# The first four batches spread over all 128 partitions, one batch per step, with their softmax through TensorE

## The chip, the core and the metric

The kernel runs on one core of a Trainium2 chip. The metric is the device time of one execution in microseconds; the time before is the median of three runs. The profile is one further execution, taken by the hardware profiler, with every instruction and every DMA packet recorded.

## What is computed

For each of 8 batches the reference takes two matrices of 4096 rows and 512 columns, both float32, forms the dot product of row i of `x` with row i of `y`, and takes the softmax of these 4096 numbers:

```python
# x, y: (8, 4096, 512) float32
gram = np.matmul(x, y.transpose(0, 2, 1))
diag = np.diagonal(gram, axis1=1, axis2=2)      # only row i with row i is used
diag = diag - diag.max(axis=-1, keepdims=True)
exp = np.exp(diag)
return exp / exp.sum(axis=-1, keepdims=True)    # (8, 4096)
```

So 134.2 MB have to be read (two inputs of 67.1 MB), each number is used once, and 0.13 MB are written.

## The kernel before

**Tiling.** The 8 batches are handled in two halves of four. In each half, partition p belongs to batch p // 32 (a quadrant of 32 partitions for each batch) and holds 128 consecutive rows of it; the starts of two neighbouring partitions lie 128 rows, 256 KB, apart in memory. A step loads 32 of these 128 rows on every partition: 64 KB per partition, 8 MB of `x` and 8 MB of `y`. Four steps make a half; there are S = 8 steps (t = 0 to 7). Column c of the tile `diag[i]` (128 x 128) takes the dot products of half i.

**Buffers.** `x` goes in turn into two tiles `xs0` and `xs1`; `y` has one tile `ys`, and a small tile `side` into which ScalarE copies the last K = 6 rows of `ys` (L123), so that they can be overwritten earlier.

**A step (L118 to L131).** The loads of `x` (L63) and `y` (L66) are issued from the queue of SyncE (SP). VectorE (DVE) multiplies the first 26 rows by `ys` (L70, 128x13312), then the last 6 by `side` (L70, 128x3072), both in place in `xs`. Then VectorE adds up 30 of the 32 products per partition (L73) and ScalarE the other two (L78). In step 0 the `x` load is cut in two: 2 rows per partition first, then 30.

**What sets the order.** The schedule is written by hand: each engine runs its instructions in the order of the source. SP runs the loads in that order too, and a load waits on SP until its buffer is free: the `x` load of step t + 2 until the sums of step t are done, the `y` load of step t + 1 until VectorE's first product of step t and the copy into `side` are done. SP's DMAs use eight completion semaphores in turn, so that a DMA can also wait for the one eight places before it. A DMA is split over 16 DMA engines, 8 partitions each; each engine works through its descriptors in the order of issue. One partition's contiguous run is one packet in the trace.

**Softmax of the first half.** After step 3, `exps` (L99) takes the largest of 128 columns (L97), the largest of each quadrant by a transposing reduction (L91), and lets ScalarE take the exponentials with their sum (L104). In step 4, ahead of its products, `normalize` (L107) adds up over the quadrant (L91), takes the reciprocal (L110) and scales (L111). TensorE has no work at all.

**The end.** Steps 6 and 7 are cut finer: in step 6 `y` comes in two parts of 16 rows, step 7 comes in parts of 16, 8, 4, 2, 1 and 1 rows, with multiply and sum in one VectorE instruction per row (`dots`, L83). Behind the last loads SP issues four DMAs of 16 KB with the result of the first half (L156). Then come the softmax of the second half and its output DMA of 64 KB, on ScalarE's queue (L158).

Of the kernel before, what the change touches and what calls it, by code (L numbers as in the profile page):

```python
# [1 line left out]

# [5 lines left out]


@with_exitstack
def kernel(
    ctx: ExitStack,
    tc: tile.TileContext,
    x: bass.AP,
    y: bass.AP,
    out: bass.AP,
):
    nc = tc.nc
    ctx.enter_context(tc.manual_schedule())  # L20
    f32 = mybir.dt.float32
    Alu = mybir.AluOpType
    Act = mybir.ActivationFunctionType
    X = mybir.AxisListType.X
    B, N, D = x.shape
    P = nc.NUM_PARTITIONS
    G = 32
    Q = P // G
    C = N // G
    R = 32  # L30
    H = R // 2
    K = 6
    W = 2
    S = B // Q * (C // R)


    xv = x.rearrange("(s b) (j c) d -> s (b j) c d", b=Q, j=G)
    yv = y.rearrange("(s b) (j c) d -> s (b j) c d", b=Q, j=G)
    ov = out.rearrange("(s b) (j c) -> s (b j) c", b=Q, j=G)

    big = ctx.enter_context(tc.tile_pool(name="big", bufs=1))
    small = ctx.enter_context(tc.tile_pool(name="small", bufs=1))


    xs = [big.tile([P, R, D], f32, name=f"xs{i}") for i in range(2)]
    ys = big.tile([P, R, D], f32, name="ys")
    side = big.tile([P, K, D], f32, name="side")

    diag = [small.tile([P, C + i], f32, name=f"diag{i}") for i in range(B // Q)]
    res = [small.tile([P, C], f32, name=f"res{i}") for i in range(B // Q)]  # L50

    def columns(t, r0, n):
        c0 = t % (C // R) * R + r0
        return slice(c0, c0 + n)

    def rows(t, r0, n):
        return xs[t % 2][:, r0 : r0 + n, :]

    def dots_of(t, r0, n):
        return diag[t * R // C][:, columns(t, r0, n)]  # L60

    def load_x(t, r0, n):
        nc.sync.dma_start(out=rows(t, r0, n), in_=xv[t * R // C, :, columns(t, r0, n), :])  # L63

    def load_y(t, r0, n):
        nc.sync.dma_start(out=ys[:, r0 : r0 + n, :], in_=yv[t * R // C, :, columns(t, r0, n), :])  # L66

    def products(t, r0, n, yt):
        xt = rows(t, r0, n)
        nc.vector.tensor_tensor(out=xt, in0=xt, in1=yt, op=Alu.mult)  # L70

    def sums(t, r0, n):
        nc.vector.tensor_reduce(out=dots_of(t, r0, n), in_=rows(t, r0, n), axis=X, op=Alu.add)  # L73

    def sums_act(t, r0, n):
        for r in range(r0, r0 + n):
            row = xs[t % 2][:, r, :]
            nc.scalar.activation(out=row, in_=row, func=Act.Copy, accum_out=dots_of(t, r, 1))  # L78

    def dots(t, r0, n):  # L80
        for r in range(r0, r0 + n):
            xt = xs[t % 2][:, r, :]
            nc.vector.scalar_tensor_tensor(  # L83
                out=xt, in0=xt, scalar=1.0, in1=ys[:, r, :], op0=Alu.mult, op1=Alu.mult,
                accum_out=dots_of(t, r, 1),
            )

    def over_quadrant(name, column, op, negate=False):

        got = small.tile([P, 1], f32, name=name)  # L90
        nc.vector.tensor_reduce(  # L91
            out=got, in_=column.to_broadcast([P, G]), axis=X, op=op, negate=negate, apply_transpose=True
        )
        return got

    def largest(out, d):
        nc.vector.tensor_reduce(out=out, in_=d, axis=X, op=Alu.max)  # L97

    def exps(i, d):  # L99
        mxp = small.tile([P, 1], f32, name=f"mxp{i}")  # L100
        largest(mxp, d)
        nmx = over_quadrant(f"nmx{i}", mxp, Alu.max, negate=True)
        sump = small.tile([P, 1], f32, name=f"sump{i}")
        nc.scalar.activation(out=res[i], in_=diag[i][:, :C], func=Act.Exp, bias=nmx, scale=1.0, accum_out=sump)  # L104
        return sump

    def normalize(i, sump):  # L107
        total = over_quadrant(f"sum{i}", sump, Alu.add)
        rc = small.tile([P, 1], f32, name=f"rc{i}")
        nc.vector.reciprocal(out=rc, in_=total)  # L110
        nc.vector.tensor_single_scalar(out=res[i], in_=res[i], scalar=rc, op=Alu.mult)  # L111

    nc.vector.addr_align(128, offset=0, max_nops=0)
    nc.scalar.addr_align(128, offset=0, max_nops=0)

    for t in range(S - 2):  # L118
        if t == 0:
            load_x(t, 0, 2)  # L120
        load_x(t, 2 if t == 0 else 0, R - 2 if t == 0 else R)
        load_y(t, 0, R)
        nc.scalar.activation(out=side, in_=ys[:, R - K :, :], func=Act.Copy)  # L123
        if t == C // R:
            normalize(0, sump)
        products(t, 0, R - K, ys[:, : R - K, :])
        products(t, R - K, K, side)
        sums(t, 0, R - W)
        sums_act(t, R - W, W)
        if t == C // R - 1:  # L130
            sump = exps(0, diag[0])  # L131

    t = S - 2
    load_x(t, 0, R)
    for r0 in (0, H):
        load_y(t, r0, H)
        products(t, r0, H, ys[:, r0 : r0 + H, :])
    sums(t, R - H // 2, H // 2)
    sums_act(t, 0, R - H // 2)

    t += 1
    r0 = 0
    for n in (16, 8, 4, 2, 1, 1):
        if r0 < R - 1:
            load_x(t, r0, max(n, 2))
        load_y(t, r0, n)
        if r0 == R - 2:
            largest(diag[1][:, C:], diag[1][:, : C - 2])
        dots(t, r0, n)
        r0 += n  # L150

    met = small.tile([P, C - R], f32, name="met")
    nc.scalar.activation(out=met, in_=diag[1][:, : C - R], func=Act.Copy)  # L153

    for p, n in ((0, G), (G, G), (2 * G, G), (3 * G, G)):
        nc.sync.dma_start(out=ov[0, p : p + n, :], in_=res[0][p : p + n, :])  # L156
    normalize(1, exps(1, diag[1][:, C - 2 :]))
    nc.scalar.dma_start(out=ov[1], in_=res[1])  # L158


# [1 line left out]
_INS = ['x', 'y']  # L162
_OUTS = [((8, 4096), 'float32')]


# [23 lines left out]
```

## Time and profile before

| | |
|---|---|
| time, median of 3 runs | 320.74 us (320.57 to 320.8) |
| profiled execution: span from the first to the last recorded event | 318.9 us |
| VectorE busy | 244.7 us (77%) |
| ScalarE busy | 42.0 us (13%) |
| TensorE | no instruction of the kernel |
| DMA queue of SP (q1) | 4080 packets, 134.29 MB, 97.8% of 16 engines' span |
| DMA queue of ScalarE (q10) | 144 packets, 0.07 MB, 0.1% |
| HBM read | 134.22 MB, 421 GB/s over the span |

The profiled execution has a span of 318.9 us; the time of a run is measured around it, and its median lies 1.8 us above the span. In the profile's lines, "x8" is a number of instructions, "busy, mean ns" their summed and mean duration, and an arrow "<-" names what ended a wait. "SPq" is SyncE's queue, where DMAs are issued. The "chain that ended last" follows the work back from the last instruction, at each step to what released it.

### The profile page before, as it was taken

To read this page: it belongs to the slowest core of one execution; us is meant where nothing else is said; L and a number is where in the kernel's file an instruction comes from. 1 tells how busy PE (TensorE), PEld (TensorE's weight loads), DVE (VectorE), ACT (ScalarE), POOL (GpSimd) and SP (SyncE) were. 2 spreads that over 40 slices of the span, in tenths; PEclk is the share of its full clock that TensorE was granted. 3 is DMA by queue.
4 is the path that set the end of the run, shared out by engine and by line. 5 is a ranking of instruction groups with operands and counts; after the bars stand their busy time and mean duration, and the time that the engine had idled before them with its cause. 6 is when DMAs were issued, how large, how long until landed. Compare 5 with 4: busy or idle time off the path is not lost.

```text
span 318.9 us, 304 instructions
## 1 busy us (share of the span) xinstructions
DVE 244.7 (77%) x96; ACT 42.0 (13%) x84; POOL 0.2 (0%) x4
## 2 busy tenths in 40 slices
DVE  0000069995899939999399994999949999996995
ACT  1000030100301003010120103000030100197000
POOL 0000000000000000000000000000000000000000
DMA  8989999999999999999999999999999899999993
GB/s 314 493 378 485 436 395 436 485 395 403 510 403 395 477 444 395 427 493 395 403 510 403 395 460 460 395 419 493 403 395 510 358 444 415 444 423 419 421 413 116
DMA packets 4226, 134.37 MB, mean 421 GB/s; under 512 B 512, under 2 KB 768, under 8 KB 1536
## 3 DMA queue, kind: packets, MB, share of 16 engines
q1 hardware_dynamic: 4080, 134.29, 97.8%
q10 hardware_dynamic: 144, 0.07, 0.1%
q14 instruction: 2, 0.02, 0.0%
HBM read 134.22 MB, written 0.13 MB: 421 GB/s over the span
## 4 chain that ended last, share of the span: by engine, by line
DMA 62%; DVE 35%; issue 2%; SPq 0%; ACT 0%; DVEq 0%
DMA ys<-in_y_dram 62%; DVE xs L70 30%; DVE diag L73 4%; DVE xs L83 0%; SPq L63 0%; DVE res L111 0%; DVE nmx L91 0%; DVE sum L91 0%; ACT res L104 0%; DVE rc L110 0%; DVE mxp L97 0%; DVEq L70 0%; SPq L66 0%; DVEq L83 0%
## 5 line engine op out<-in xcount | busy, mean ns | idle before, releaser
L70 DVE TENSOR_TENSOR xs<-xs,ys 128x13312 f32<-128x13312 f32 (+1 forms) x8 | 101.4, 12690 | 66.5 <-DMA ys<-in_y_dram 66.5
L73 DVE TENSOR_REDUCE diag<-xs 128x30 f32<-128x15360 f32 (+1 forms) x7 | 101.3, 14477 | 0.2
L78 ACT ACTIVATE xs<-xs 128x512 f32<-128x512 f32 x36 | 22.2, 616 | 111.0 <-DVE xs L70 111.0
L123 ACT ACTIVATE side<-ys 128x3072 f32<-128x3072 f32 x6 | 16.6, 2764 | 124.0 <-DMA ys<-in_y_dram 124.0
L83 DVE SCALAR_TENSOR_TENSOR xs<-xs,ys 128x512 f32<-128x512 f32 x32 | 19.9, 686 | 3.3 <-DMA ys<-in_y_dram 3.3
L70 DVE TENSOR_TENSOR xs<-xs,side 128x3072 f32<-128x3072 f32 x6 | 20.1, 3351 | 0.0
L78 ACT ACTIVATION_READ_ACCUMULATOR xs<-xs 128x1 f32 x36 | 6.7, 186 | 0.0
L104 ACT ACTIVATE res<-diag,nmx 128x128 f32<-128x128 f32 x2 | 0.8, 402 | 37.6 <-DVE nmx L91 37.6
L83 DVE DVE_READ_ACCUMULATOR xs<-xs,ys 128x1 f32 x32 | 2.6, 81 | 0.0
L123 ACT ACT_TABLE_LOAD x1 | 1.3, 1283 | 1.2 <-PEq L173 1.2
L91 DVE TRANSPOSE_TENSOR_REDUCE sum<-sump 128x1 f32<-128x32 f32 x2 | 0.4, 212 | 1.2 <-ACT res L104 1.2
L111 DVE TENSOR_SCALAR res<-res,rc 128x128 f32<-128x128 f32 x2 | 0.6, 286 | 0.1
L97 DVE TENSOR_REDUCE mxp<-diag 128x1 f32<-128x128 f32 (+1 forms) x2 | 0.4, 220 | 0.1
L91 DVE TRANSPOSE_TENSOR_REDUCE nmx<-mxp 128x1 f32<-128x32 f32 x2 | 0.4, 212 | 0.1
L110 DVE RECIPROCAL rc<-sum 128x1 f32<-128x1 f32 x2 | 0.3, 164 | 0.1
L104 ACT ACTIVATION_READ_ACCUMULATOR res<-diag,nmx 128x1 f32 x2 | 0.4, 186 | 0.0
L97 DVE TENSOR_REDUCE diag<-diag 128x1 f32<-128x126 f32 x1 | 0.3, 284 | 0.1
L153 ACT ACTIVATE met<-diag 128x96 f32<-128x96 f32 x1 | 0.3, 282 | 0.0
L173 POOL MEMSET const-bfloat16-1.0<- 128x1 bf16 x1 | 0.1, 102 | 0.0
L173 POOL MEMSET const-uint8-127<- 128x1 uint8 x1 | 0.1, 102 | 0.0
L173 POOL MEMSET const-float32-0.0<- 128x1 f32 x1 | 0.1, 99 | 0.2 <-issue 0.2
L173 POOL MEMSET const-float32-1.0<- 128x1 f32 x1 | 0.1, 99 | 0.0
## 6 DMA issues: line engine op xcount, KB each, us to landing
ys<-in_y_dram SPq DMA_DIRECT2D x3, 4096.0 KB, 16.0
xs<-in_x_dram SPq DMA_DIRECT2D x1, 7680.0 KB, 21.8
xs<-in_x_dram SPq DMA_DIRECT2D x1, 4096.0 KB, 14.9
xs<-in_x_dram SPq DMA_DIRECT2D x1, 2048.0 KB, 20.5
ys<-in_y_dram SPq DMA_DIRECT2D x1, 2048.0 KB, 17.2
xs<-in_x_dram SPq DMA_DIRECT2D x3, 512.0 KB, 22.1
xs<-in_x_dram SPq DMA_DIRECT2D x1, 1024.0 KB, 19.3
ys<-in_y_dram SPq DMA_DIRECT2D x1, 1024.0 KB, 21.3
```

The costliest lines, as they stand in the source:

```text
L70: nc.vector.tensor_tensor(out=xt, in0=xt, in1=yt, op=Alu.mult)
L73: nc.vector.tensor_reduce(out=dots_of(t, r0, n), in_=rows(t, r0, n), axis=X, op=Alu.add)
L78: nc.scalar.activation(out=row, in_=row, func=Act.Copy, accum_out=dots_of(t, r, 1))
L83: nc.vector.scalar_tensor_tensor(out=xt, in0=xt, scalar=1.0, in1=ys[:, r, :], op0=Alu.mult, op1=Alu.mult, accum_out=dots_of(t, r, 1),)
L91: nc.vector.tensor_reduce(out=got, in_=column.to_broadcast([P, G]), axis=X, op=op, negate=negate, apply_transpose=True)
L97: nc.vector.tensor_reduce(out=out, in_=d, axis=X, op=Alu.max)
L104: nc.scalar.activation(out=res[i], in_=diag[i][:, :C], func=Act.Exp, bias=nmx, scale=1.0, accum_out=sump)
L110: nc.vector.reciprocal(out=rc, in_=total)
L111: nc.vector.tensor_single_scalar(out=res[i], in_=res[i], scalar=rc, op=Alu.mult)
L123: nc.scalar.activation(out=side, in_=ys[:, R - K :, :], func=Act.Copy)
L153: nc.scalar.activation(out=met, in_=diag[1][:, : C - R], func=Act.Copy)
L173: nc = _bacc.Bacc("TRN2", target_bir_lowering=False, num_devices=1)
```

## The change

Only the first half (steps 0 to 3) is laid out anew. The second half is as before.

- **Loads.** Step t (0 to 3) takes batch t alone, over all 128 partitions: partition p takes the 32 rows from 32 p, so that the 8 MB of a load are one contiguous piece of memory and neighbouring partitions lie 64 KB apart. In step 0 partition p takes row p (column 0) and the 31 rows from 128 + 31 p; both `x` and `y` come in two DMAs there, of 1 row (2 KB per partition, 256 KB contiguous in all) and of 31 rows (62 KB per partition).
- **Softmax of the first half.** A batch is now a group of 32 columns on all 128 partitions. `exps_of_four` takes the largest of each group and partition, the largest of each quadrant by a transposing reduction, spreads these over 16 columns with a mask, and lets a matmul with a matrix of ones bring all four quadrants' values to every partition (`all_q`, in PSUM); VectorE takes the largest of four with a minus sign. ScalarE takes the exponentials in four instructions of 32 columns, and a second matmul with ones adds their sums up over the partitions (`total`, in PSUM). `normalize_four` takes the reciprocal and scales.
- **Constants.** GpSimd fills `ones` and `mask` at the start.
- **Output of the first half.** Three DMAs instead of four: 31 columns (124 B per partition), one column (4 B per partition), and three batches of 32 columns (three runs of 128 B per partition).

```diff
-    xv = x.rearrange("(s b) (j c) d -> s (b j) c d", b=Q, j=G)
-    yv = y.rearrange("(s b) (j c) d -> s (b j) c d", b=Q, j=G)
...
+    def of_rows(v, t, r0, n):
+        if t >= Q:
+            return v[Q:].rearrange("b (j c) d -> (b j) c d", j=G)[:, columns(t, r0, n), :]
+        if t > 0:
+            return v[t].rearrange("(p c) d -> p c d", p=P)[:, r0 : r0 + n, :]
+        if r0 == 0:
+            return v[0][:P].rearrange("(p c) d -> p c d", p=P)
+        return v[0][P:].rearrange("(p c) d -> p c d", p=P)[:, r0 - 1 : r0 - 1 + n, :]
...
+    def exps_of_four():
+        mxp = small.tile([P, Q], f32, name="mxp0")
+        nc.vector.tensor_reduce(out=mxp, in_=groups(diag[0][:, :C]), axis=X, op=Alu.max)
+        mxq = small.tile([P, Q], f32, name="mxq0")
+        nc.vector.tensor_reduce(
+            out=mxq, in_=mxp.unsqueeze(2).to_broadcast([P, Q, G]), axis=X, op=Alu.max, apply_transpose=True
+        )
+        one_each = small.tile([P, Q, Q], f32, name="one_each")
+        nc.vector.tensor_tensor(
+            out=one_each, in0=mxq.unsqueeze(1).to_broadcast([P, Q, Q]), in1=mask, op=Alu.mult
+        )
+        all_q = psum.tile([P, Q * Q], f32, name="all_q")
+        nc.tensor.matmul(all_q, lhsT=ones, rhs=one_each.rearrange("p q g -> p (q g)"), start=True, stop=True)
+        nmx = small.tile([P, Q], f32, name="nmx0")
+        nc.vector.tensor_reduce(
+            out=nmx, in_=all_q.rearrange("p (q g) -> p g q", q=Q), axis=X, op=Alu.max, negate=True
+        )
+        sump = small.tile([P, Q], f32, name="sump0")
+        for g in range(Q):
+            nc.scalar.activation(
+                out=res[0][:, g * R : (g + 1) * R], in_=diag[0][:, g * R : (g + 1) * R], func=Act.Exp,
+                bias=nmx[:, g : g + 1], scale=1.0, accum_out=sump[:, g : g + 1],
+            )
+        total = psum.tile([P, Q], f32, name="total")
+        nc.tensor.matmul(total, lhsT=ones, rhs=sump, start=True, stop=True)
+        return total
+
+    def normalize_four(total):
+        rc = small.tile([P, Q], f32, name="rc0")
+        nc.vector.reciprocal(out=rc, in_=total)
+        nc.vector.tensor_tensor(
+            out=groups(res[0]), in0=groups(res[0]), in1=rc.unsqueeze(2).to_broadcast([P, Q, R]), op=Alu.mult
+        )
...
+    nc.gpsimd.memset(ones, 1.0)
+    nc.gpsimd.memset(mask, 0.0)
+    for q in range(Q):
+        nc.gpsimd.memset(mask[q * G : q * G + 1, q, :], 1.0)
...
     for t in range(S - 2):
-        if t == 0:
-            load_x(t, 0, 2)
-        load_x(t, 2 if t == 0 else 0, R - 2 if t == 0 else R)
-        load_y(t, 0, R)
+        for load in (load_x, load_y):
+            if t == 0:
+                load(t, 0, 1)
+            load(t, 1 if t == 0 else 0, R - 1 if t == 0 else R)
...
-            normalize(0, sump)
+            normalize_four(total)
...
-            sump = exps(0, diag[0])
+            total = exps_of_four()
...
-    for p, n in ((0, G), (G, G), (2 * G, G), (3 * G, G)):
-        nc.sync.dma_start(out=ov[0, p : p + n, :], in_=res[0][p : p + n, :])
+    nc.sync.dma_start(out=out[0][P:].rearrange("(p c) -> p c", p=P), in_=res[0][:, 1:R])
+    nc.sync.dma_start(out=out[0][:P].rearrange("(p c) -> p c", p=P), in_=res[0][:, :1])
+    nc.sync.dma_start(out=out[1:Q].rearrange("b (p c) -> p b c", p=P), in_=groups(res[0])[:, 1:, :])
```

## The prediction, made before the changed kernel was run

> **What bounds the kernel now.** I read the page first: span, DMA queues, and the chain that ended last.
>
> ```profile
> span 318.9 us, 304 instructions
> q1 hardware_dynamic: 4080, 134.29, 97.8%
> DMA 62%; DVE 35%; issue 2%; SPq 0%; ACT 0%; DVEq 0%
> ```
>
> The chain gives 35% to VectorE, but the second line says that all 16 DMA engines were busy for 97.8% of the span. Both can be true only if the chain's VectorE pieces lie beside other transfers. The chain in order of time shows that:
>
> ```profile
> 56.57 24.46 DMA ys<-in_y_dram
> 81.03 0.03 issue
> 81.06 0.02 DVEq L70
> 81.08 0.04 issue
> 81.12 14.04 DVE xs L70
> 95.16 0.02 SPq L66
> 95.18 0.03 issue
> 95.21 24.52 DMA ys<-in_y_dram
> ```
>
> One step lasts from 56.57 to 95.21, that is 38.64 us, for 16.78 MB: 434 GB/s. While VectorE multiplies (14.04 us), the next `x` is on its way. A `y` issued at 95.21 lands 24.5 us later although its own bytes take 38.64 / 2 = 19.3 us: for 5.2 us it stands behind `x`. So the DMA engines never run dry, with 5 us to spare, and only what changes their work, their start or what follows the last byte can move the end.
>
> The DMA packet records in the trace (start, duration, size of every packet) show how even this is:
>
> ```
> size of packet   count   mean ns   lowest   highest
> 65536 B           1536    2420.7     2418      2509
> 61440 B            128    2267.1     2267      2272
>  4096 B, at start  128     234.1      156       655
>  4096 B, in step 7 384     162.6               172
>  2048 B            256      86.7       84        98
>   512 B (result)   128      27.0       27        29
>     4 B (semaphore) 496      9.1        7        14
> ```
>
> Large packets run at 27.1 GB/s on every engine, and 16 x 27.1 = 434. The exception is the very first load (2 rows, 4 KB per partition). The same size with the same 256 KB between partitions took 162.6 ns in step 7 and 234.1 ns at the start, and 52 of the 128 took over 200 ns. The next row of evidence is when that load has landed:
>
> ```profile
> xs<-in_x_dram SPq DMA_DIRECT2D x1, 512.0 KB, 4.1
> ```
>
> (DMA issues in the first 3 us; the last number is us from issue to landing.) In the packet records its first packet starts at 12.82 us of the recorder's clock and its last ends at 15.50, 2.68 us later, where eight packets of 162.6 ns would be 1.30. The engines go over to the 30-row load between 14.61 and 15.50, a spread of 0.89. At the other end the last packets of `y` end between 323.76 and 324.52, a spread of 0.76: as all engines have equal work, what the slowest loses at the start is never made up.
>
> **The change part by part.** The sum is made against the profiled execution: 318.9 us of span and 1.8 us around it, against the median of 320.74. I leave the 1.8 us as they are.
>
> *Steady loads.* Steps 1 to 3 move the same packets of 64 KB, from partitions 64 KB apart instead of 256 KB. At 256 KB the lowest packet of 65536 B takes 2418 ns and the mean is 2420.7, so at most 2.7 ns of a packet can depend on addresses: 48 packets on an engine (steps 1 to 3) x 2.7 ns = 0.13 us of possible gain. For a loss the trace has no row at 64 KB; the largest excess of a packet is 2509 - 2418 = 91 ns, and 48 x 91 ns = 4.4 us is the far bound. I take 0, as 256 KB, 2 KB and 4 KB runs all reach their rates in steady state.
>
> *Step 0, warm.* Before: 8 packets each of 4, 60 and 64 KB on an engine: 8 x (162.6 + 2267 + 2421) = 38.80 us. After: 8 x (86.7 + 2343 + 86.7 + 2343) = 38.87 us, with 63488 B / 27.1 = 2343 ns. That is +0.08 us, with the additional semaphore packet (9 ns). The additional issue on SP takes 0.4 us (0.87 us for the first two); SP has 40 us until its next wait. A 1-row load is 0.7 us of work and the next issue comes 0.43 us later, so no gap opens.
>
> *Step 0, cold.* Here the time is decided. Upper bound of the gain: no slow packet. The 16 engines' first packets start within 0.28 us; then 8 x 86.7 ns = 0.69 us, so the slowest would be done at 12.82 + 0.28 + 0.69 = 13.79. The rest of step 0 is 8 x 4687.7 = 37.50 us before and 8 x 4772.7 = 38.18 us after. End of step 0: 53.00 before, 51.97 after, -1.03 us. Lower bound: every cold delay stays (1.39 us on the slowest), which gives the warm sum, +0.08 us; and if both 1-row loads pay it, +1.4 us. Why I go towards the gain: the pitch is not the cause, since step 7 has it too, and the 64 KB packets of the first `y`, as freshly touched, show at most 91 ns. What the slow packets have in common is that each is a small first touch of a place 256 KB from the next. The new first load touches one 256 KB piece, with four 2 KB rows side by side. I take a quarter to a third of the delay as left: -0.75 us; the `y` row load comes when the engines are deep in their queues, and I charge it nothing more.
>
> *The softmax in the middle.* The gap into which it must fit:
>
> ```profile
> 192.04 0.28 DVE L97 TENSOR_REDUCE mxp<-diag 128x1 f32<-128x128 f32 x1
> 193.63 0.29 DVE L111 TENSOR_SCALAR res<-res,rc 128x128 f32<-128x128 f32 x1
> 197.22 14.02 DVE L70 TENSOR_TENSOR xs<-xs,ys 128x13312 f32<-128x13312 f32 x1 [3.30 <-DMA ys<-in_y_dram]
> 211.31 0.33 SPq L66 DMA_DIRECT2D ys<-in_y_dram  x1
> ```
>
> Before, it takes 1.9 us of 5.1. After: maximum 0.28, transposed maximum 0.21, mask product 0.16 to 0.29, two matmuls of which the trace has no row (between the shortest VectorE row, 0.16, and the ACT table load, 1.28; I take 0.7 each, a middle), maximum of four 0.16 to 0.28, four exponentials at 0.25 + 0.19 (a 128-column one starts its accumulator read 0.31 after its own start, and that read takes 0.19) = 1.8, reciprocal 0.16, scaling 0.29, and some 0.6 of hand-overs: 5.3 us, from 3.8 to 6.6. So VectorE's first product of step 4 may start up to 1.5 us late. Behind it wait the `y` of step 5 (issued 211.31) and the sums that free `xs0`. The `x` before it keeps the DMA engines busy until about 216.5, so the cover is 5.2 us; for `x` of step 6 it is about the same. Cost: 0; without the cover, 1.5 us. The copy into `side` waits on ScalarE behind the exponentials, but its reader comes 14 us later. `x` of step 5 is issued when the sums end, ahead of all this. The constants on GpSimd are needed 190 us later: 0.
>
> *The output.* The three DMAs stand in SP's queue and in every engine's ring where four stood, behind the last `y`, so no load is behind them. Each engine gets 40 small writes instead of 8. A packet costs between 9.1 ns (4 B) and 27 ns (512 B): 0.36 to 1.08 us, where it was 0.22. They have time until the final output reaches the same engines:
>
> ```profile
> 313.40 0.69 DVE L83 SCALAR_TENSOR_TENSOR xs<-xs,ys 128x512 f32<-128x512 f32 x1 [0.24 <-DMA ys<-in_y_dram]
> 316.48 0.38 ACTq L158 DMA_DIRECT2D out_dram<-res  x1
> out_dram<-res ACTq DMA_DIRECT2D x1, 64.0 KB, 1.6
> ```
>
> In the packet records the last small write ends at 324.73 and the final output starts at 328.42: 3.7 us of cover. Cost 0; the point where it costs is 8 x 27 ns + 3.7 us spread over 40 packets, some 98 ns each.
>
> A rule speaks against this part. The Trainium skill, "DMA: Bandwidth & Descriptors", section "Specifications", gives 512 B as the least size for line rate and says that below it the engine does read-modify-write. No run here shows a result write under 512 B. If such a write cost two full turns of 27 ns, an estimate from this row and the page, the 40 would take 2.2 us and still be covered.
>
> A second rule speaks for the change: the same page, section "Latency and other measured facts", reports power-of-two row pitches from 512 KiB up as slow and advises contiguous tiles. The trace has 256 KB, and shows 2420.7 ns against a floor of 2418, so nothing is left to win there in steady state.
>
> The sum: -0.75 (cold, with the warm +0.08 in it) + 0 + 0 + 0 = -0.75 us, to 318.1 us of span and 320.0 us of time.
>
> **The rivals.** What a measurement of this kernel can tell from no change is about 0.2%, 0.64 us.
>
> *The first load stays cold.* The slowness may belong to the first packets whatever they read. For it: it is over within 2.7 us of the first packet. Against it: 76 of the 128 had little of it. Between half and all of the delay left: -0.5 to +0.1 us, 320.2 to 320.8.
>
> *Slower: the small writes end the kernel.* 512 of the 640 packets are written as pieces of 124 or 128 B, or of 4 B beside each other, and if each costs over 98 ns, the final output and the closing wait stand behind them. At 150 ns, 40 x 150 = 6.0 us against a cover of 3.9: +2.1 us, 322.8; at 120 ns, +0.9, 321.6. Against it: the 4 B semaphore writes at 9.1 ns, though these carry no result.
>
> *Slower: two cold loads instead of one*, or packets hindered at 64 KB: +0.7 to +1.4 us, 321.4 to 322.1. Against it: 91 ns at most in the first `y` packets.
>
> **How the numbers follow.** The contiguous first load is freed of most of its delay: 0.50, at -1.03 to -0.5 us. It stays cold: 0.27. Small writes: 0.12. Two cold loads or pitch: 0.11. The likeliest gives 320.0. Its own range is 319.7 to 320.25; the range for all reaches from 319.5 (the bound of -1.03, with 0.13 of the steady loads) to 321.6, which takes in the second case and the lower part of the slower ones. Faster by over 0.2%, 0.46: nearly the whole first case, since the -0.75 lies beyond the 0.64 and only its upper end does not. Same, 0.31: the second and that end. Slower, 0.23.
>
> **What would show it right or wrong.** In the DMA issues of the changed kernel: the 1-row `x` load lands under 3.2 us after its issue (right) or at 3.5 and more (cold). The chain keeps its step of 38.6 us in steps 1 to 3; a longer one says that the 64 KB pitch costs. The first product of step 4 starts within 2 us of the landing of its `y`, and the `y` behind it still lands at the step's pace; if not, the softmax came out of its cover. The result's three DMAs land before the final one is issued; if they land after it, the second rival holds. I am wrong altogether if the span moves while step lengths, first landing and tail stay.

## The result: slower, 324.19 us against 320.75 us

The changed kernel took 324.19 us (median of four runs, 323.64 to 324.48) where the kernel before took 320.75 us: a ratio of 1.0101, with a 95% interval of 1.0089 to 1.0113. That lies above the predicted range of 319.5 to 321.6 us.

The page of the changed kernel shows the same kind of kernel, bound by its DMA engines:

```profile
span 322.7 us, 329 instructions
q1 hardware_dynamic: 4720, 134.29, 96.8%
DMA 61%; DVE 34%; issue 2%; SPq 0%; ACT 0%; DVEq 0%
```

The 640 additional packets are those of the finer cut (128) and of the output (512). The chain in order of time gives the step and the last load:

```profile
57.01 24.49 DMA ys<-in_y_dram
81.59 14.04 DVE xs L80
95.68 24.51 DMA ys<-in_y_dram
...
294.51 19.21 DMA ys<-in_y_dram
```

The step is 95.68 - 57.01 = 38.67 us, against 38.64. Before, the last `y` was

```profile
294.06 19.25 DMA ys<-in_y_dram
```

It now lands at 294.51 + 19.21 = 313.72, against 313.31: 0.4 us late, and the chain was 0.44 late already at 57.01. So what the start cost, it cost once, and the rest of the loads took what they took before. The rest of the loss, over 3 us, comes after the last load. The timeline there and the DMA issues of the last 23 us (last number: us from issue to landing):

```profile
313.82 0.69 DVE L93 SCALAR_TENSOR_TENSOR xs<-xs,ys 128x512 f32<-128x512 f32 x1 [0.28 <-DMA ys<-in_y_dram]
...
316.97 0.38 ACTq L211 DMA_DIRECT2D out_dram<-res  x1
```

```profile
out_dram<-res ACTq DMA_DIRECT2D x1, 64.0 KB, 4.9
out_dram<-res SPq DMA_DIRECT2D x1, 48.0 KB, 11.2
out_dram<-res SPq DMA_DIRECT2D x1, 15.5 KB, 10.4
out_dram<-res SPq DMA_DIRECT2D x1, 0.5 KB, 13.5
```

The final output is issued 0.49 us later than before (316.97 against 316.48), and then lands after 4.9 us instead of 1.6. 0.5 + 3.3 = 3.8 us, which is the whole difference of the spans (322.7 - 318.9). SP's waits show where: at the end of the kernel SP waits for outputs, before (L184) and after (L237); the numbers are us in total, waits, and the longest.

```profile
SPq L184 <- DMA out_dram<-res: 7.0, 2, 3.7
SPq L237 <- DMA out_dram<-res: 6.9, 2, 5.5
```

The longest wait grew from 3.7 to 5.5 us. The total did not grow, so this row alone would not have shown the loss; the landing does.

Here is what makes this hard to see beforehand. The DMA packet records show the new small writes as quick: 13 ns each (124 B and 128 B) and 9 ns (4 B), the last one begun before the final output's first packet. By these records the engines were done with them 3.6 us before the final output began. But with issue times of 306.8 and 309.3, the 0.5 KB and the 48 KB DMA land at 320.3 and 320.5, some 6 us after their packets.

The middle gap, for the softmax of the first half:

```profile
192.57 0.29 DVE L122 TENSOR_REDUCE mxp<-diag 128x4 f32<-128x128 f32 x1
193.54 0.61 PE L132 MATMUL all_q<-one_each,ones 128*128 128x16 f32 x2 [193.54 <-DVE one_each L128]
196.69 0.29 DVE L150 TENSOR_TENSOR res<-res,rc 128x128 f32<-128x128 f32 x1
197.69 14.03 DVE L80 TENSOR_TENSOR xs<-xs,ys 128x13312 f32<-128x13312 f32 x1 [0.71 <-DMA ys<-in_y_dram]
```

It ends at 196.98, and the `y` of step 4 lands at 173.07 + 24.52 = 197.59: 0.6 us to spare.

### The profile page after: what moved, and what is told of

It reads as the page before. It is cut to its first block, busy times and chain, and to the rows that moved or that the text cites. A ratio compares the mean times of both kernels' runs of the same rounds, so it can differ in the third digit from the quotient of the medians.

```text
span 322.7 us, 329 instructions
## 1 busy us (share of the span) xinstructions
PE 1.2 (0%) x4; PEld 1.0 (0%) x4; DVE 245.0 (76%) x97; ACT 42.8 (13%) x90; POOL 0.8 (0%) x10
## 4 chain that ended last, share of the span: by engine, by line
DMA 61%; DVE 34%; issue 2%; SPq 0%; ACT 0%; DVEq 0%
DMA ys<-in_y_dram 61%; DVE xs L80 30%; DVE diag L83 4%; DVE xs L93 0%; SPq L73 0%; SPq L76 0%; DVE res L158 0%; DVE sum L101 0%; DVE nmx L101 0%; ACT res L114 0%; DVE rc L157 0%; DVE mxp L107 0%; DVEq L80 0%; DVEq L93 0%
## 5 line engine op out<-in xcount | busy, mean ns | idle before, releaser
L139 ACT ACTIVATE res<-diag,nmx 128x32 f32<-128x32 f32 x4 | 1.2, 310 | 16.7 <-DVE nmx L134 16.7
```

Source lines behind the costliest of these rows:

```text
L139: nc.scalar.activation(out=res[0][:, g * R : (g + 1) * R], in_=diag[0][:, g * R : (g + 1) * R], func=Act.Exp, bias=nmx[:, g : g + 1], scal ...
```

## The experiments

**Theories.** A: the small pieces of the output are counted as landed late, and the final output lands behind them. B: the end is late for another reason. For the start, the prediction's premise (scattered first touches are slow) stands against theory C (the delay belongs to the start and moves on to whatever is read then).

### Which output DMA? (e1 to e4)

e2, e3 and e4 each leave out one of the three output DMAs; e1 keeps all three and issues them some 90 us earlier.

```diff
# e1_out_early: in the loop over steps, behind load_y
+        if t == C // R + 1:
+            nc.sync.dma_start(out=out[0][P:]..., in_=res[0][:, 1:R])
+            nc.sync.dma_start(out=out[0][:P]..., in_=res[0][:, :1])
+            nc.sync.dma_start(out=out[1:Q]..., in_=groups(res[0])[:, 1:, :])
# e2_no_4B
-    nc.sync.dma_start(out=out[0][:P].rearrange("(p c) -> p c", p=P), in_=res[0][:, :1])
# e3_no_128B
-    nc.sync.dma_start(out=out[1:Q].rearrange("b (p c) -> p b c", p=P), in_=groups(res[0])[:, 1:, :])
# e4_no_124B
-    nc.sync.dma_start(out=out[0][P:].rearrange("(p c) -> p c", p=P), in_=res[0][:, 1:R])
```

> The changed kernel without the output DMA of one column (128 runs of 4 B beside each other; column 0 of batch 0 is not written). Theory A in the form that the 4 B runs are the slow ones: final output lands after some 1.6 to 2 us, time 320.9 to 321.3. Theory A in the form that the 128 B runs are slow, or that the number of runs decides: 512 of 640 runs are left, so 2.6 of the 3.3 us stay, 323.5. Theory B: 324.2.

> The changed kernel without the output DMA of three batches (384 runs of 128 B; batches 1 to 3 are not written). Theory A with 4 B runs as the slow ones: still 323.5 to 324.2. Theory A by number of runs: 256 of 640 are left, 3.3 x 0.4 = 1.3 us stay, 322.2. With the 128 B runs as the slow ones: 320.9. Theory B: 324.2.

> The changed kernel without the output DMA of 31 columns (128 runs of 124 B; rows 128 to 4095 of batch 0 are not written). In the profile of the changed kernel this DMA lands 10.4 us after its issue, which is 314.7 and in front of the two others, so theory A in its 4 B or 128 B form: 323.5 to 324.2. By number of runs: 512 of 640 are left, 323.5. If the runs of 124 B, which begin at no multiple of 128 B, were the slow ones: 320.9. Theory B: 324.2.

| kernel | time, us | ratio to before, 95% interval | final output, issue to landing |
|---|---|---|---|
| changed | 324.19 | 1.0101 (1.0089 to 1.0113) | 4.9 us |
| e2, no 4 B runs | 321.19 | 1.0011 (1.0001 to 1.0020) | 1.6 us |
| e3, no 128 B runs | 323.91 | 1.0097 (1.0075 to 1.0120) | 4.6 us |
| e4, no 124 B runs | 324.10 | 1.0096 (1.0079 to 1.0113) | 4.5 us |

It is the DMA of 0.5 KB, the smallest of the kernel: without it 3.0 of 3.4 us are gone. The 512 runs of 124 and 128 B cost nothing that these runs resolve (e3 and e4 lie 0.1 to 0.3 us below the changed kernel, whose own runs span 0.8). In e2 the final output is back at its old landing:

```profile
out_dram<-res ACTq DMA_DIRECT2D x1, 64.0 KB, 1.6
out_dram<-res SPq DMA_DIRECT2D x1, 48.0 KB, 8.0
out_dram<-res SPq DMA_DIRECT2D x1, 15.5 KB, 10.3
```

e1 asked whether the cost can be hidden in the middle of the kernel.

> The changed kernel with its three output DMAs of the first half issued behind the y load of step 5 instead of behind the last load; nothing is left out. Theory A (small pieces: the 640 runs under 512 B take 13 ns each on the DMA engines but are counted as landed only microseconds later, and the final output lands behind them): the final output lands 1.6 us after its issue as before (4.9 in the changed kernel), time 324.2 - 3.3 = 320.9 us. Theory B (the end is late for another reason than these writes): the final output still lands about 4.9 us after its issue, 324.2 us. If the pieces also hold up loads that stand behind them, the step after them is longer than 38.7 us and the time lies between.

Not at this place, and the run went beyond all that was expected: 327.79 us, a ratio of 1.0219 (1.0191 to 1.0246), 3.6 us worse than with the DMAs at the end. The final output does land after 1.6 us again, as theory A says, but now loads stand behind the small writes, and they are held up. The windows of e1 around that place (columns: stretch, its length, busy us of PE, PEld, DVE, ACT, POOL, PE clock, DMA share, GB/s; a packet counts whole in the window where it starts, so the share of long ones can exceed 1):

```profile
230.00:235.00 5.00, 0.00 (x0) 0.00 (x0) 1.06 (x1) 0.00 (x0) 0.00 (x0) 1.00 0.80 332
235.00:240.00 5.00, 0.00 (x0) 0.00 (x0) 3.48 (x1) 2.77 (x1) 0.00 (x0) 1.00 1.73 271
240.00:245.00 5.00, 0.00 (x0) 0.00 (x0) 5.00 (x1) 0.00 (x0) 0.00 (x0) 1.00 0.54 144
```

The same windows of the changed kernel have 472, 446 and 433 GB/s. The packet records of e1 show 64 KB packets of up to 8959 ns there instead of 2418; the excess of the 30 long ones adds up to 6.3 us per engine, on average over the 16. e1 moved all three output DMAs; that the stall is the 0.5 KB one's is read from their landings. The 15.5 KB DMA, issued just ahead of it, lands after 24.8 us like the `y` before them; the 0.5 KB one lands after 30.3, and its 16 completion signals come over 7.2 us, those of the 15.5 KB one over about 1.5. So this DMA of 0.5 KB costs about 6 us of all DMA engines. At the end of the kernel 3.3 us of that show; the rest, an estimate of 2.7 us, lies beside the last softmax.

### Small, or side by side? (e5, e6, e13 to e15; e12)

All but e12 leave out the 124 B runs, as e4 did (324.1 us), and change only where, or how broad, the 128 small runs are.

```diff
# e5: 4 B runs, 128 B apart (e14: 64 B, e15: 32 B apart)
-    nc.sync.dma_start(out=out[0][:P].rearrange("(p c) -> p c", p=P), in_=res[0][:, :1])
+    nc.sync.dma_start(out=out[0].rearrange("(p c) -> p c", p=P)[:, :1], in_=res[0][:, :1])
# e6: 64 B runs beside each other (e13: 32 B, with 8 for 16)
+    nc.sync.dma_start(out=out[0][: 16 * P].rearrange("(p c) -> p c", p=P), in_=res[0][:, :16])
```

> The changed kernel without the output DMA of 31 columns, and with the 128 runs of 4 B written 128 B apart instead of beside each other (rows of batch 0 get column 0's values at every 32nd place, the others are not written). To be compared with the run that left out the 31 columns alone (324.1 us, final output landing 4.5 us after its issue). Theory A1 (a 4 B run is slow by its size): 324.1 us, 4.5 us to landing. Theory A2 (the runs are slow because they lie beside each other, 128 of them in 512 B, written by 16 DMA engines): some 321.0 us and 1.6 us to landing.

> The changed kernel without the output DMA of 31 columns, and with 128 runs of 64 B beside each other (16 columns, 8 KB in all) where the 128 runs of 4 B were; the places written in batch 0 hold other values than the reference. Theory A1 by size: 64 B is sixteen times 4 B and half of the 128 B runs that cost nothing, so 321.0 us, or up to 322.5 if the cost goes by the step below 128 B. Theory A2 (beside each other): if any neighbours hinder each other, still some 324; if only those within a common short piece of memory (under 64 B) do, 321.0.

> The changed kernel without the output DMA of 31 columns, with 128 runs of 32 B beside each other (8 columns, 4 KB in all) in place of the 128 runs of 4 B; batch 0 then holds other values. 4 B runs landed late (4.5 us) beside each other and not 128 B apart; 64 B runs beside each other did not. If what matters is that a run covers less than the 64 B piece it lies in while a neighbour writes into the same piece: still late, though with 2 writers in a piece instead of 16 perhaps 2 to 3 us. If the piece is 32 B: 1.6 us.

> The changed kernel without the output DMA of 31 columns, with the 128 runs of 4 B written 64 B apart (the rest of batch 0 is not written). If only neighbours within 64 B hinder each other: final output lands in 1.6 us, span 319. If neighbours within 128 B do: later, 2 us and more.

> The changed kernel without the output DMA of 31 columns, with the 128 runs of 4 B written 32 B apart (the rest of batch 0 is not written). If the common piece is 32 B: 1.6 us. If it is 64 B, each piece has 2 writers: between 1.6 and 4.5 us, as for the runs of 32 B.

| small runs | time, us | final output, issue to landing |
|---|---|---|
| e4: 4 B, side by side (4 B apart) | 324.10 | 4.5 us |
| e15: 4 B, 32 B apart | 320.96 (one run; before beside it 320.89) | 1.6 us |
| e14: 4 B, 64 B apart | 320.86 (one run) | 1.6 us |
| e5: 4 B, 128 B apart | 321.00, ratio 1.0007 (0.9997 to 1.0016) | 1.6 us |
| e13: 32 B, side by side | 320.92 (one run) | 1.6 us |
| e6: 64 B, side by side | 321.24, ratio 1.0013 (1.0004 to 1.0023) | 1.6 us |

The landing of the final output alone could leave some 3 us unseen beside the softmax. The landing of the small DMA itself rules that out (e4, then e15):

```profile
out_dram<-res SPq DMA_DIRECT2D x1, 0.5 KB, 14.9
out_dram<-res SPq DMA_DIRECT2D x1, 0.5 KB, 10.3
```

In e5 and e14 it lands after 10.3 us too, as does the DMA of 8 KB or 4 KB in e6 and e13. In the completion records its 16 signals come over 5.8 us in e4 and over 1.0 us in e15.

So the size of a write is innocent here: 4 B runs cost nothing when they lie 32 B or more apart. What costs is that the runs lie closer than that, several in the same 32 B of memory. Between 4 B and 32 B no run looks closer, so the piece that they share may be smaller, and why such writes wait for each other is not shown.

e12 puts the suspect into the kernel before, with no TensorE, no new layout and no 124 or 128 B runs:

```diff
-    for p, n in ((0, G), (G, G), (2 * G, G), (3 * G, G)):
+    for p, n in ((16, 16), (G, G), (2 * G, G), (3 * G, G)):
         nc.sync.dma_start(out=ov[0, p : p + n, :], in_=res[0][p : p + n, :])
+    nc.sync.dma_start(out=out[0][:P].rearrange("(p c) -> p c", p=P), in_=res[0][:, :1])
```

> The kernel before, with 128 runs of 4 B beside each other added to its output DMAs (they go to the first 512 B of batch 0, and the result of partitions 0 to 15 is not written). Theory A2 (runs of 4 B beside each other are slow, whatever kernel they stand in): the final output lands about 4.6 us after its issue instead of 1.6, time 320.75 + 3.1 = 323.9. If the changed kernel's late end needs anything else of that kernel (TensorE, the layout, the 124 B or 128 B runs): 320.8.

324.03 us, 1.0100 (1.0082 to 1.0118), as forecast by theory A2. The side-by-side 4 B runs suffice:

```profile
out_dram<-res ACTq DMA_DIRECT2D x1, 64.0 KB, 5.4
out_dram<-res SPq DMA_DIRECT2D x3, 16.0 KB, 6.4
out_dram<-res SPq DMA_DIRECT2D x1, 8.0 KB, 10.3
out_dram<-res SPq DMA_DIRECT2D x1, 0.5 KB, 8.0
```

### The change with this taken out (e7, e8)

e7 keeps the whole change and turns column 0 by one transposing VectorE instruction in the middle gap, so that it leaves in 4 runs of 128 B. e8 lays step 0 out like steps 1 to 3, with the cut of before, and writes the first half in one DMA of 512 runs of 128 B.

```diff
# e7_column_turned
+        nc.vector.transpose(out=turned, in_=res[0][:, :R])     # end of normalize_four
-    nc.sync.dma_start(out=out[0][:P].rearrange("(p c) -> p c", p=P), in_=res[0][:, :1])
+    nc.sync.dma_start(out=out[0][:P].rearrange("(q j) -> q j", j=G), in_=turned[0:P:G, :])
# e8_even_batches: of_rows(v, t < Q) is always the line below; the cut of step 0 and the output are not shown
+        return v[t].rearrange("(p c) d -> p c d", p=P)[:, r0 : r0 + n, :]
```

> The changed kernel, complete, with column 0 turned into four rows of 32 values by one more VectorE instruction in the middle gap (32x32 transposes), so that it is written in 4 runs of 128 B instead of 128 of 4 B. Theory A in its 4 B form: as the run without the 4 B runs, 321.2 us, final output landing 1.6 us after its issue; what is then left against the kernel before (0.4 us) is the start. If the cost lay in anything else that came with column 0: 324.

> The changed kernel, complete, with step 0 laid out as steps 1 to 3 (32 contiguous rows of 64 KB per partition) and cut as before the change: x in 2 + 30 rows, y in one DMA. Its output is then 512 runs of 128 B and none of 4 or 124 B. Theory A in its 4 B form: no late landing, 320.7 to 321.2 us, where 320.7 says that the 1-row loads cost the 0.4 us and 321.2 that the layout does. Theory A by number of runs under 512 B: 512 of 640 left, 323.5.

321.30 us (1.0015, 1.0006 to 1.0025) and 321.14 us (1.0009, 1.0000 to 1.0019). The repair takes 2.9 us off the changed kernel; what is left of the idea is no gain but a loss of 0.4 to 0.5 us (for e8 the interval begins at no change). No complete version here beats the kernel before.

### The start (e9, e10, e11)

```diff
# e9_first_together: the kernel before, first load from one piece of 512 KB
+        if t == 0 and r0 == 0:
+            nc.sync.dma_start(out=rows(t, r0, n), in_=x[0][: n * P].rearrange("(p c) d -> p c d", p=P))
+            return
# e10_one_row: the kernel before, x of step 0 in 1 + 31 rows
-            load_x(t, 0, 2)
-        load_x(t, 2 if t == 0 else 0, R - 2 if t == 0 else R)
+            load_x(t, 0, 1)
+        load_x(t, 1 if t == 0 else 0, R - 1 if t == 0 else R)
# e11_uncut: the kernel before, x of step 0 in one DMA
-        if t == 0:
-            load_x(t, 0, 2)
-        load_x(t, 2 if t == 0 else 0, R - 2 if t == 0 else R)
+        load_x(t, 0, R)
```

> The kernel before, with the first x load (2 rows per partition, 4 KB each) read from 512 KB in one piece instead of from places 256 KB apart; columns 0 and 1 of the first half then hold other products than the reference. Premise of the prediction (scattered first touches are what is slow): the load lands in some 3.2 us instead of 4.1, the 60 KB packets stay at 2267 ns, time 320.75 - 0.75 = 320.0. Theory C (a first touch costs wherever it comes, so the delay moves on to the next load): the 60 KB packets, now first touches, take more than 2267 ns in their first row, and the time stays within 320.5 to 321.2.

> The kernel before, with x of step 0 cut in 1 + 31 rows instead of 2 + 30, places 256 KB apart as they were; nothing is left out. Premise of the prediction: cold delay stays as the places stay apart, 320.7. Theory C: the same, 320.7 to 321.2. If the 1-row size by itself is what costs the changed kernels their 0.4 us: 321.1.

> The kernel before, with x of step 0 in one DMA of 32 rows; nothing is left out. Theory C: the first 64 KB packets carry the delay, 2700 ns and more instead of 2418, and the time is within 0.3 us of 320.75. If only short packets suffer (a long one hides a first touch, as the first y load of the kernel before suggests): 320.75 - 0.5 = 320.2.

| kernel | time, us | excess over 27.1 GB/s in step 0, per engine, and in which packets |
|---|---|---|
| before | 320.75 | 0.66 us in the 4 KB packets, 0.02 later |
| e9 | 321.02, 1.0009 (1.0000 to 1.0018) | 0.44 in 4 KB, 0.14 later |
| e10 | 320.85, 1.0001 (0.9993 to 1.0010) | 0.30 in 2 KB, 0.33 later |
| e11 | 320.81, 0.9999 (0.9990 to 1.0008) | 0.65 in 64 KB |
| changed | 324.19 | 0.35 in 2 KB, 0.34 in 62 KB |
| e7 | 321.30 | 0.51 in 2 KB, 0.31 in 62 KB |
| e8 | 321.14 | 0.71 in 4 KB, 0.35 in 60 KB |

The last column is summed from the packet records of one profile each (duration minus size / 27.1 GB/s). 0.09 us of it belongs to every load of 1 or 2 rows even undisturbed, at 86.7 and 162.6 ns a packet. The delay is there whatever is read first, 0.6 to 1.1 us here: cut small, about half of it or more shows in the small packets; uncut, the first sixteen 64 KB packets take 3010 ns on average instead of 2418. A contiguous first load doesn't avoid it either: in e9 the 4 KB packets take 206 ns on average, and the load lands after 4.6 us, where the premise asked for 3.2 and the kernel before has 4.1. The rows can't be ranked: the eleven profiles with the start of the changed kernel (it, e1 to e7 and e13 to e15) scatter from 0.4 to 0.9 us. So the premise falls. Theory C holds in that no cut and no place got rid of the delay; that it moves on as a fixed amount is not shown.

## Why the prediction was wrong, by its own steps

**The sum.** -0.75 us was forecast and +3.4 measured. 3.0 of the 4.2 us between them go with the 0.5 KB DMA (e2), priced at 0; the other 1.2 are the gain at the start that did not come and a loss there instead.

**The output: the step that failed.** It priced a small write by the time it holds a DMA engine, "0.36 to 1.08 us", and that was right in its own terms: 32 packets of 13 ns and 8 of 9 ns are 0.49 us on an engine. But the kernel's end waits for landings, and no row of the trace before had several writes into the same 32 B. Its bounds, 9.1 and 27 ns, were packet durations only, and so it left out what decides. The rival with the small writes named the right place and the right result, the final output and the closing wait behind them, though not by the mechanism that was measured: its point of decision (98 ns a packet) and its price (+2.1 us at 150 ns) were in the wrong unit, and it had 0.12. The mechanism it missed cost 3.3 us in the profile.

The rule from the Trainium skill that was weighed there (512 B as the least size for line rate, read-modify-write below it) names no price. Small packets are indeed below the line rate here, 128 B in 13 ns being 9.8 GB/s, but the runs of 124, 128, 64 and 32 B, and of 4 B laid 32 B or more apart, show no cost in time: their final output lands at the old 1.6 us. Whether an engine reads before such a write, no run shows. Nearer is another section of the same page, "DMA: Bandwidth & Descriptors", "Queues, rings and completion order": a completion signal lands only after every earlier write of that DMA engine, across its queues. The final output agrees: it goes through another queue (ScalarE's), its own packets take 27 ns each, and it lands 3.3 us late behind SP's writes. Of its 16 completion signals in the changed kernel eight come at 318.4 to 318.5 us, 1.5 us after its issue, the other eight at 319.1 to 321.9; the last signal of the small writes comes at 320.4. That order does not explain why loads behind the small writes are held up in e1; that stays open.

**Step 0, cold.** -0.75 us was forecast; the `y` of step 0 landed 0.47 us later (before, then changed: 42.33 and 42.80):

```profile
1.65 40.68 DMA ys<-in_y_dram
2.13 40.67 DMA ys<-in_y_dram
```

The first load became quicker by a third of what was asked (4.1 to 3.8 us, where under 3.2 was wanted), and lies above the 3.5 us that were the mark for "cold". Its size alone would do: one row from places 256 KB apart lands after 3.6 us (e10).

```profile
xs<-in_x_dram SPq DMA_DIRECT2D x1, 256.0 KB, 3.8
```

What it saved reappeared in the 62 KB packets behind it, 2634 ns for the first sixteen against 2342 undisturbed. A reading under the upper bound was wrong as well: "the 16 engines' first packets start within 0.28 us" counts sixteen packets, not sixteen engines. At the end of that time, 13.10 us of the recorder's clock, ten packets are in work at once, and sixteen only from about 14.1. Argued, not tested: one engine in each trace also serves an 8 KB instruction fetch then (1058 ns before, 1359 ns in the changed kernel), and an engine whose first data packet comes only after it (13.91 and 14.55) would be the last to go over to the large load (15.50 and 15.45); the packet records used here do not name the engine. If so, the forecast took that straggler for a cold one. How late the `y` of step 0 lands differs from profile to profile even with the same start: between 42.3 and 43.0 us in the eleven named above.

**Steady loads.** Right: 38.67 us a step against 38.64, so 64 KB between partitions neither gains nor costs. **The softmax in the middle.** Right, cost 0: 4.4 us from 192.57 to 196.98, where 5.3 was estimated and 3.8 to 6.6 bounded; the two matmuls took 0.6 us each, where 0.7 was taken. **Step 0, warm**, +0.08 us, is too small to be seen.

## What to carry to other kernels

A write has two prices: the time its packet holds a DMA engine, and the time until it has landed; at the end of a kernel, and ahead of loads in the same ring, the second one counts, and the write's own packet durations don't show it. Before a layout is chosen for its reads, look at how its results leave: one value of 4 B per partition, side by side in memory, is the pattern to avoid (turn it first, one VectorE instruction here, or let each partition own 32 B or more). The slow stretch at the start was not won by reading something else first.

## What was not expected of the hardware

- 128 writes of 4 B beside each other (512 B in all) held the 16 DMA engines up for some 6 us each, on average, when loads stood behind them (64 KB packets of up to 8959 ns), though their own packets took 9 ns; 32 B apart they cost nothing.
- The late landing crosses queues: the final output on ScalarE's queue landed after 4.5 to 5.4 us instead of 1.6.
- The first step's loads lose 0.4 to 1.1 us per engine against 27.1 GB/s in every profile, at every cut that was tried, from 2 KB to 64 KB packets.
